# Moving the dots of the adaLN parameters between the stages of a two-layer decoder trunk

## The chip, the cores and the metric

The kernel runs on one core of one Trainium2 chip. A core has TensorE (PE; its weight loads, shown apart as PEld, overlap the products), VectorE (DVE), ScalarE (ACT), GpSimd (POOL) and SyncE (SP, which here only issues DMAs). The metric is device microseconds (us) of one execution; a kernel's time is the median of its runs.

## The reference

Two layers work on x of 512 positions by 1024 features, float32, one sequence. Both parts of a layer start with an RMS norm that is scaled and shifted by parameters computed from a vector c (adaLN):

```python
c_act = silu(c)
for l in range(2):
    mod = (c_act @ w_ada + b_ada)[:, None, :]
    sh1, sc1, g1, sh2, sc2, g2 = jnp.split(mod, 6, axis=-1)       # 1024 values each
    h = rmsnorm(x, norm1_w) * (1 + sc1) + sh1
    u = h @ w_in
    u_pool, u_conv, b_conv, c_conv, q, k, v, gate_logits = jnp.split(u, offsets, axis=-1)
    y_pool = pool_mixer(u_pool, pool_w, pool_scale)               # 256 wide
    y_conv = b_conv * causal_short_conv(c_conv * u_conv, conv_w)  # 256 wide
    q, k = rope(rmsnorm(q)), rope(rmsnorm(k))                     # 8 heads of 64
    o = moba_attention(q, k, v)                                   # blocks of 256 keys
    gates = sigmoid(gate_logits)                                  # 3 x 1024
    merged = (gates[:, :, 0] * (y_pool @ p_pool) + gates[:, :, 1] * (y_conv @ p_conv)
              + gates[:, :, 2] * (y_attn @ p_attn))
    x = x + g1 * (merged @ w_out)
    h2 = rmsnorm(x, norm2_w) * (1 + sc2) + sh2
    x = x + g2 * ((silu(h2 @ w_gate) * (h2 @ w_up)) @ w_down)     # 2816 wide
```

Each of the six parameters of a layer is a vector of 1024 sums over 1024 products. Sc1 and sh1 are wanted when the layer starts, g1 by the projection after the gates, sc2 and sh2 by the second norm, g2 by the first down projection.

## The kernel before

**Layout and products.** Activations lie feature by position: x is eight tiles of 128 features by 512 positions. A float32 product is made of three products of rounded halves: each operand is split into a rounded part and the rest (hi and lo), and `mm3` issues hi x hi, hi x lo and lo x hi into one accumulator (`matmul`, L149). There are four single accumulators in PSUM (`ps_mm`) and two double ones (`ps_pair`). All matmuls and some other instructions are pinned in program order; the rest the Tile framework's scheduler may move on their engine.

**The weights** come as one stream in a planned order, eight 128x128 blocks (512 KB) at a time. `next_w` keeps up to `ahead_now` of them loaded ahead. `load_w` has SP issue the DMA (L232) into a tile named `raw`, of which there are three (`RAW`); ACT copies the rounded part (L325, `whi`) and DVE subtracts (L328, `wlo`), five buffers each. The split frees the raw tile, a matmul frees whi and wlo. In the feed-forward part, gate and up weights are summed in memory by POOL's accumulating DMAs (L254, L256) into tiles named `w`, of which there are six; they are then split by the same two lines.

**The dots.** The adaLN parameters are not made on PE. For 128 values at a time `ada_step` has SP load 512 KB of `w_ada`, transposed on the host, and DVE multiplies by silu(c) and sums along the row in one instruction (L374). Its tile is a raw one where `early` is true, else a w one (`w4`). `ada_tasks` lists the eight dots of a part, at a cost of 1.2 each, and `ada_end`, at 0.2, which adds the bias and, for a scale, folds in the norm's weight. Layer 0's scale and shift 1 are computed apart (`ada_first`), at the start.

**The order of work** is written by hand around PE. Each 2048 output columns of matmuls (four `mm3` of 512) make one `tick()`. A tick advances the `fibers` (attention) and runs tasks from a queue, `bulk`, by a credit that grows by `bulk_rate[0]` with each tick; `flush_bulk()` runs all that is left:

```python
def ada_step(l, part, j, early):
    aw = wp.tile([P, D], F32, tag="raw", name=nm("raw"), bufs=RAW) if early else w4([P, D])
    nc.sync.dma_start(aw, ada[l, part, j])
    pin(ada_dot(aw, l, part, j))
...
gains = ada_tasks(l, (G1,)) if l > 0 else []
bulk.extend(gains[:4])
k_ps = wide()
...
bulk.extend(ada_tasks(l, (G1, SC2, SH2)[l:], True))
bulk_rate[0] = (0.5, 0.35)[l]
```

**The stages of a layer**, with what runs as bulk in them:

- *The loop along k* (L723 to L744) makes q and the first three of the six pool and convolution tiles, and goes along the contraction because the norm's output comes one feature tile at a time. In layer 1 `second()` (L738) finishes the norm of the second half of the positions.
- *Convolution, k and v*: three products by `feature_tile`, then `wide()` twice, for k and for v. The pool and convolution chains run as bulk on DVE; `flush_bulk()` ends the convolution's, k's and v's part. In layer 1 the eight dots of G1 are here (L849): four in k's part, four in v's.
- *Convolution and pool products* (L888 to L899): the convolution's first tile, two pool products, the convolution's second tile. L890 multiplies the first into the convolution's output, `cv`.
- *Gates and attention* (L901 on): 24 gate products, each through Tanh (L909) and `gated` (L914), with the products of the three branches; attention's units run between them as fibers. A unit is 128 queries of a pair of heads: scores, maxima and gate sums on DVE (L602 to L610), exponentials on ACT (L612, L614), scaling on DVE (L616 to L619), transposes on PE (L155), products with v. As bulk run, in early (raw) tiles, 24 dots in layer 0 (G1, SC2, SH2, at a rate of 0.5) and 16 in layer 1 (SC2, SH2, at 0.35).
- *The projection* with `tail`, adding to x by L954 (`residual`), with the dots of G2 as bulk in w tiles.
- *Feed-forward* in four parts, `PARTS` (L47): products of gate and up, most of them in pairs by a Strassen-Winograd scheme (`glu_pair`, Silu in L1087 to L1089), then the part's down products, added to x by L954. At the start of each down stage the bulk rate is set to 1.5, and halfway through it to 0. Part 0 of layer 0 holds the dots of layer 1's SC1 and SH1 (L1126); parts 1 and 2 hold none. The last part's down products run in `tail` with layer 1's first norm (L1139 to L1146).

Of the kernel before, what the change touches and what calls it, by code (L numbers as in the profile page):

```python
# [24 lines left out]
L = 2  # L25
# [21 lines left out]
PARTS = ((3, 1, 1), (0, 0, 3), (0, 0, 2), (0, 0, 3))  # L47

SUMS_AHEAD = 4

RAW, BIG = 3, 46

# [5 lines left out]
SH1, SC1, G1, SH2, SC2, G2 = range(6)  # L58
# [19 lines left out]
def hybrid_trunk(ctx, tc, xT, ws, ada, cols, pool_w, qk_w, crow, pos, con, out):  # L78
    nc = tc.nc
    V, A, T = nc.vector, nc.scalar, nc.tensor  # L80
# [20 lines left out]
    def ps_mm():  # L101
        return psum.tile([P, S], F32, tag="mm", name=nm("mm"), bufs=4)
# [16 lines left out]
    bulk = deque()  # L119
    bulk_rate, credit = [0.0], [0.0]  # L120
# [23 lines left out]
    def drain():  # L144
        while fibers:
            tick()
# [202 lines left out]
    def next_w(ahead=None):  # L349
        ahead = ahead_now[0] if ahead is None else ahead  # L350
        while at[0] < len(items) and len(loaded) <= ahead:
            loaded.append(load_w())
        return loaded.popleft()
# [55 lines left out]
    def ada_tasks(l, parts, early=False):  # L409
        out = []  # L410
        for part in parts:
            for j in range(KT):
                out.append((1.2, lambda part=part, j=j: ada_step(l, part, j, early)))
            out.append((0.2, lambda part=part: ada_end(l, part)))
        return out
# [90 lines left out]
    def split_from(src, scale=None):  # L506

        hi, lo = bigt(), bigt()
        if scale is None:
            A.activation(hi, src, AF.Copy)  # L510
            V.tensor_sub(lo, src, f32(hi))  # L511
        else:
            A.activation(hi, src, AF.Copy, scale=scale)
            V.scalar_tensor_tensor(lo, src, scale, f32(hi), op0=ALU.mult, op1=ALU.subtract)
        return hi, lo

    def second(nrm, l, i, bank):

        hold[0] = None
        nrm.stat(BLOCK, S, bank)  # L520
        for k, lo, hi in HALVES[3:] + REST:
            nrm.apply(l, i, k, lo, hi)
# [192 lines left out]
    for l in range(L):  # L715
# [7 lines left out]
        for n, (k, lo, hi) in enumerate([(k, 0, S) for k in range(KT)] if l == 0 else HALVES + REST):  # L723
            if l == 0:
                if k + 3 < KT:
                    first.append(ada_first_load(k + 3))
                if k + 2 < KT:
                    ada_first(k + 2, first[k + 2], SC1)
                    ada_first(k + 2, first[k + 2], SH1)
                    norm.first_scaled(k + 2)  # L730
                    norm.first_hi(k + 2)
                loaded.append(load_w())
                if k + 2 < KT:
                    norm.first_lo(k + 2)
            if k not in held:
                held[k] = next_w(0 if l == 0 else None)
            if l > 0 and n == 1:
                second(norm, l, 0, bank)  # L738
            w = held[k]
            h = norm.k(k)  # L740
            for t in range(lo // P, hi // P):
                mm3(q_ps[t], cut(h, slice(None), slice(t * P, (t + 1) * P)), wrow(w, 0), k == 0, k == KT - 1)
            for z in range(3):
                mm3(f_ps[z][:, lo:hi], wblk(w, 4 + z), cut(h, slice(None), slice(lo, hi)),  # L744
                    k == 0 and lo == 0, k == KT - 1)
# [8 lines left out]
        def feature_tile(o, w):  # L754
            for k in range(KT):
                mm3(o, wblk(w, k), norm.k(k), k == 0, k == KT - 1)
# [56 lines left out]
        cv = {}  # L813
# [32 lines left out]
            if j == 1:  # L846
                bulk.append((0, lambda: pool_chain(1, pool1)))

        gains = ada_tasks(l, (G1,)) if l > 0 else []  # L849
        bulk.extend(gains[:4])  # L850
        k_ps = wide()
        for t in range(TT):
# [32 lines left out]

        m01, y_attn = [], []
        fibers.append([3, attention(l, qk, v, nrq, prq, y_attn)])
        pb = ps_mm()  # L888
        feature_tile(pb, next_w())
        V.tensor_mul(cv[0], pb, cv[0])  # L890
        y_conv.append(split_from(cv[0]))
        for j in range(2):
            pp = ps_mm()
            mm3(pp, (pw["h"][:, j, :], pw["l"][:, j, :]), pooled[j], True, True)
            y_pool.append(split_from(pp, scale=col(C_PS + j)))
        pb = ps_mm()
        feature_tile(pb, next_w())
        V.tensor_mul(cv[1], pb, cv[1])
        y_conv.append(split_from(cv[1]))  # L899

        bulk.extend(ada_tasks(l, (G1, SC2, SH2)[l:], True))  # L901
        bulk_rate[0] = (0.5, 0.35)[l]
        ahead_now[0] = 3

        def gate():
# [190 lines left out]
        for part, (along, single, pairs) in enumerate(PARTS):  # L1096
            act = []
            nk = along + single + 2 * pairs
            if along:
                held = {}  # L1100
                for n, (k, lo, hi) in enumerate(HALVES + REST):
                    if n == 1:
                        second(norm, l, 1, bank)
                        table(AF.Silu, norm.y[:, 0:1])
                    if k not in held:
                        held[k] = next_w()
                    for z in range(2 * FA):
                        mm3(f_ps[z][:, lo:hi], wblk(held[k], z), cut(norm.k(k), slice(None), slice(lo, hi)),
                            k == 0 and lo == 0, k == KT - 1)
                    if k >= HK:  # L1110
                        make_forms(k - HK)
                del held
                for z in range(FA):
                    glu(f_ps[z], f_ps[FA + z])
            for _ in range(single):
                wg = next_w()
                g = ps_mm()
                feature_tile(g, wg)
                u = ps_mm()
                feature_tile(u, next_w())  # L1120
                glu(g, u)
            bulk_rate[0] = 0.0
            for _ in range(pairs):
                glu_pair()
            if part == 0 and l + 1 < L:
                bulk.extend(ada_tasks(l + 1, (SC1, SH1)))  # L1126
            bulk_rate[0] = 1.5
            blk = Blocks(nk, 4)
            if part + 1 < len(PARTS):
                for n in range(KT):  # L1130
                    if n == KT // 2:
                        bulk_rate[0] = 0.0
                    o = ps_mm()
                    for k in range(nk):
                        mm3(o, blk(n, k), act[k], k == 0, k == nk - 1)
                    residual(n, o, 0, S, G2)
            elif l + 1 == L:
                tail(lambda k: act[k], blk, G2, nk, None, True)
            else:  # L1139
                flush_bulk()  # L1140
                drain()
                n1 = Norm()
                table(AF.Abs_reciprocal_sqrt, f32(act[-1][1])[:, 0:1])
                scratch = ps_pair()
                bank = scratch[:, 1]
                tail(lambda k: act[k], blk, G2, nk, n1, False, lead(n1, l + 1, 0, bank), 4)  # L1146
                norm = n1
# [100 lines left out]
```

## Time and profile before

| | |
|---|---|
| time, median of 3 runs | 1480.35 us |
| lowest and highest | 1479.25 and 1482.27 us |
| the profiled execution | 1480.46 us |
| its span in the profile | 1478.7 us |
| ACT and POOL busy | 666.3 us (45%), 105.8 us (7%) |
| DMA | 217.19 MB, 147 GB/s on average |

The span goes from the first instruction to the last; the time of the execution holds some 1.8 us around it. All times within the kernel are from the start of the span.

A row of a timeline gives start, length, engine, line, operation, output and inputs with their form and a count (instructions of one kind behind one another are drawn together). In brackets stand the idle time of the engine ahead of it and who ended it. "mm" and "pair" are accumulators, "big" a tile of 128x512, "tmp" a scratch tile, "in_ws" the stream of weights in memory, "in_ada" the transposed w_ada. Rows that sum the waits give engine, tile and line, releaser, and then total, number and largest. A table of windows gives, for each stretch, its length and each engine's busy time with its instructions, then the granted clock of TensorE (1.00 is full speed), the share of the DMA engines and GB/s. A row of the DMA issues gives queue, count, size and the time from issue to landing.

DVE's largest groups by line are the weight splits (L328), 284.7 + 86.7 us from raw and from w tiles, the dots (L374), and the residuals (L954) with 62.0 us; ACT's largest are the splits' first halves (L325), 248.8 + 76.2 us.

### The profile page before, as it was taken

The page shows a single profiled execution, that of the slowest core. Times are in us where ns is not written, and L with a number is a line of the kernel's source. Part 1 is how long each engine was busy: PE and PEld are TensorE (multiplying, and loading weights), DVE is VectorE, ACT ScalarE, POOL GpSimd, SP SyncE. Part 2 cuts the span into 40 slices and gives each one's busy share as a digit, 9 for nine tenths or more (in the row PEclk, how much of TensorE's full clock was granted, in tenths as well). Part 3 has the DMA queues.
Part 4 walks back from the last instruction along what each step waited for, and adds up shares of the span by engine and source line. Part 5 has one row for each costly group of instructions (what it writes and reads, how often), then busy time and mean ns, then how long its engine had stood idle before and what let it go on. Part 6 is the DMA issues. An engine that isn't in the chain of part 4 may idle for free.

```text
span 1478.7 us, 21940 instructions
## 1 busy us (share of the span) xinstructions
PE 1456.7 (99%) x8443; PEld 1268.0 (86%) x8443; DVE 1052.2 (71%) x1855; ACT 666.3 (45%) x1138; POOL 105.8 (7%) x157
## 2 busy tenths in 40 slices
PE   8999999999999999999999999999999999999999
PEld 6888787778988998989988877778889889989997
DVE  7976887758686876767666777776586757657672
ACT  4634555443453352535444345455335525434350
POOL 0000000001100211210000000000010102111200
PEclk9999999999999999999999999999999999999999
DMA  9514433365337775744334443333462436637431
GB/s 346 199 73 159 141 136 134 115 227 148 109 114 221 207 190 174 198 113 117 114 109 146 155 143 126 102 114 128 143 193 81 141 114 167 191 89 196 131 105 65
DMA packets 84409, 217.19 MB, mean 147 GB/s; under 512 B 10832, under 2 KB 23760, under 8 KB 84304
## 3 DMA queue, kind: packets, MB, share of 16 engines
q1 hardware_dynamic: 67456, 177.37, 35.2%
q0 software_dynamic: 16128, 37.76, 11.6%
q8 instruction: 66, 1.08, 0.3%
q10 hardware_dynamic: 720, 0.66, 0.1%
q14 instruction: 39, 0.32, 0.1%
HBM read 213.65 MB, written 2.10 MB: 146 GB/s over the span
## 4 chain that ended last, share of the span: by engine, by line
PE 84%; DVE 8%; DMA 3%; ACT 3%; issue 1%; SPq 0%; DVEq 0%; ACTq 0%
PE mm L149 72%; PE pair L149 11%; DMA raw<-in_ws 2%; DVE wlo L328 2%; PE mm L155 1%; ACT whi L325 1%; DMA w<-in_ada 1%; DVE w L374 1%; DVE raw L374 1%; ACT tmp L612 0%; DMA x<-in_xT 0%; ACT tmp L614 0%; DVE big L914 0%; SPq L232 0%; DVE big L929 0%
## 5 line engine op out<-in xcount | busy, mean ns | idle before, releaser
L149 PE MATMUL mm<-big,whi 128*128 128x512 f32 (+1 forms) x4362 | 1083.3, 340 | 5.6 <-DVE tmp L1081 2.5
L149 PEld LDWEIGHTS mm<-big,whi 128*128 128x128 f32 x4362 | 746.0, 190 | 93.6 <-DVE tmp L1081 4.1
L149 PE MATMUL mm<-big,wlo 128*128 128x512 f32 (+1 forms) x2181 | 736.1, 337 | 0.0
L149 PEld LDWEIGHTS mm<-big,wlo 128*128 128x128 f32 x2181 | 413.9, 190 | 44.7
L325 ACT ACTIVATE whi<-raw 128x1024 fp32r<-128x1024 f32 (+2 forms) x240 | 248.8, 1039 | 298.3 <-PE mm L149 231.1
L328 DVE TENSOR_TENSOR wlo<-raw,whi 128x1024 fp32r<-128x1024 f32 (+2 forms) x240 | 284.7, 1193 | 81.9 <-ACT whi L325 81.0
L325 ACT ACTIVATE whi<-w 128x1024 fp32r<-128x1024 f32 x72 | 76.2, 1059 | 147.8 <-PE mm L149 107.7
L954 DVE SCALAR_TENSOR_TENSOR x<-mm,mod,x 128x512 f32<-128x512 f32 (+1 forms) x90 | 62.0, 689 | 101.4 <-PE mm L149 101.3
L254 POOL DMA_DIRECT2D w<-in_ws x72 | 48.5, 683 | 982.1 <-DVE w L374 377.3
L328 DVE TENSOR_TENSOR wlo<-w,whi 128x1024 fp32r<-128x1024 f32 x72 | 86.7, 1220 | 31.0 <-ACT whi L325 30.2
L149 PE MATMUL pair<-whi,big 128*128 128x512 f32 x224 | 76.7, 390 | 0.0
L256 POOL DMA_DIRECT2D w<-in_ws x72 | 64.6, 923 | 153.1 <-DMA w<-in_ws 136.3
L149 PE MATMUL pair<-big,whi 128*128 128x256 f32 (+1 forms) x376 | 74.0, 294 | 0.0
L374 DVE SCALAR_TENSOR_TENSOR w<-w,csil 128x1024 f32<-128x1024 f32 x56 | 66.9, 1220 | 9.5 <-DMA w<-in_ada 9.3
L149 PEld LDWEIGHTS pair<-big,whi 128*128 128x128 f32 x376 | 60.4, 191 | 2.2
L149 PE MATMUL mm<-whi,big 128*128 128x512 f32 x160 | 57.2, 394 | 1.7 <-ACT big L497 1.4
L149 PE MATMUL pair<-big,wlo 128*128 128x256 f32 (+1 forms) x188 | 55.3, 294 | 0.0
L511 DVE TENSOR_TENSOR big<-tmp,big 128x512 fp32r<-128x512 f32 x48 | 33.0, 690 | 24.3 <-ACT big L510 23.4
L149 PEld LDWEIGHTS pair<-whi,big 128*128 128x128 f32 x224 | 42.1, 188 | 8.7
L374 DVE SCALAR_TENSOR_TENSOR raw<-raw,csil 128x1024 f32<-128x1024 f32 x40 | 48.4, 1218 | 1.2 <-DMA raw<-in_ada 1.2
L914 DVE SCALAR_TENSOR_TENSOR big<-big,mm 128x512 f32<-128x512 f32 x48 | 32.6, 682 | 21.5 <-PE mm L149 21.1
L149 PE MATMUL pair<-wlo,big 128*128 128x512 f32 x112 | 43.6, 390 | 0.0
(187 smaller groups left out, 1251.5 us busy)
## 6 DMA issues: line engine op xcount, KB each, us to landing
raw<-in_ws SPq DMA_DIRECT2D x146, 512.0 KB, 3.4
w<-in_ws POOLq DMA_DIRECT2D x144, 256.0 KB, 4.6
w<-in_ada SPq DMA_DIRECT2D x56, 512.0 KB, 5.3
raw<-in_ada SPq DMA_DIRECT2D x40, 512.0 KB, 3.2
raw<-in_ws SPq DMA_DIRECT2D x64, 256.0 KB, 4.2
raw<-in_ws SPq DMA_DIRECT2D x24, 384.0 KB, 3.5
raw<-in_ws SPq DMA_DIRECT2D x16, 448.0 KB, 5.3
raw<-in_ws SPq DMA_DIRECT2D x36, 128.0 KB, 3.0
```

The source lines that it names most:

```text
L149: tc.keep_in_program_order(T.matmul(*a, **k))
L155: tc.keep_in_program_order(T.transpose(*a))
L254: nc.gpsimd.dma_start(dst, self.source(0, 1))
L256: nc.gpsimd.dma_start(dst, self.source(*other), accum_op=ALU.add)
L325: A.activation(hi[:, :n], raw[:, :n], AF.Copy)
L328: ins = V.tensor_sub(lo[:, :n], raw[:, :n], f32(hi)[:, :n])
L374: return V.scalar_tensor_tensor(aw, aw, 1.0, csil, op0=ALU.mult, op1=ALU.mult, accum_out=mod[l][:, part, j:j + 1])
L511: V.tensor_sub(lo, src, f32(hi))
L914: V.scalar_tensor_tensor(sg, sg, 1.0, branch, op0=ALU.add, op1=ALU.mult)
L954: V.scalar_tensor_tensor(x[k][:, lo:hi], src, mod[l][:, part, k:k + 1], x[k][:, lo:hi], op0=ALU.mult, op1=ALU.add)
```

## The change

Dots move to other stages, and the convolution and pool products change places:

- G1's eight dots of layer 0 go from the gate stage into the k and v stage, in w tiles, as they already are in layer 1. Layer 0's gate stage keeps SC2's and SH2's 16, at a rate of 0.35 in place of 0.5.
- The 16 dots of layer 1's SC2 and SH2 go from layer 1's gate stage into w tiles earlier in the program: the first five (`AHEAD2`) into the down stage of part 2 of layer 0, the other three of SC2 with its `ada_end` into the last down stage of layer 0, at a rate of 0.8, and SH2's eight into layer 1's loop along k, behind `second()`, at 0.6. Layer 1's gate stage has none left.
- The order convolution 0, pool 0, pool 1, convolution 1 becomes convolution 0, pool 0, convolution 1, pool 1. The weights' order in the stream stays.

No product, dot or transfer is added or taken away.

```diff
--- before.py
+++ after.py
@@ -47,6 +47,7 @@
 PARTS = ((3, 1, 1), (0, 0, 3), (0, 0, 2), (0, 0, 3))
 
 SUMS_AHEAD = 4
+AHEAD2 = 5
 
 RAW, BIG = 3, 46
 
@@ -736,6 +737,8 @@
                 held[k] = next_w(0 if l == 0 else None)
             if l > 0 and n == 1:
                 second(norm, l, 0, bank)
+                bulk.extend(later)
+                bulk_rate[0] = 0.6
             w = held[k]
             h = norm.k(k)
             for t in range(lo // P, hi // P):
@@ -846,7 +849,7 @@
             if j == 1:
                 bulk.append((0, lambda: pool_chain(1, pool1)))
 
-        gains = ada_tasks(l, (G1,)) if l > 0 else []
+        gains = ada_tasks(l, (G1,))
         bulk.extend(gains[:4])
         k_ps = wide()
         for t in range(TT):
@@ -885,21 +888,18 @@
 
         m01, y_attn = [], []
         fibers.append([3, attention(l, qk, v, nrq, prq, y_attn)])
-        pb = ps_mm()
-        feature_tile(pb, next_w())
-        V.tensor_mul(cv[0], pb, cv[0])
-        y_conv.append(split_from(cv[0]))
         for j in range(2):
+            pb = ps_mm()
+            feature_tile(pb, next_w())
+            V.tensor_mul(cv[j], pb, cv[j])
+            y_conv.append(split_from(cv[j]))
             pp = ps_mm()
             mm3(pp, (pw["h"][:, j, :], pw["l"][:, j, :]), pooled[j], True, True)
             y_pool.append(split_from(pp, scale=col(C_PS + j)))
-        pb = ps_mm()
-        feature_tile(pb, next_w())
-        V.tensor_mul(cv[1], pb, cv[1])
-        y_conv.append(split_from(cv[1]))
-
-        bulk.extend(ada_tasks(l, (G1, SC2, SH2)[l:], True))
-        bulk_rate[0] = (0.5, 0.35)[l]
+
+        if l == 0:
+            bulk.extend(ada_tasks(l, (SC2, SH2), True))
+        bulk_rate[0] = 0.35
         ahead_now[0] = 3
 
         def gate():
@@ -1122,8 +1122,13 @@
             bulk_rate[0] = 0.0
             for _ in range(pairs):
                 glu_pair()
-            if part == 0 and l + 1 < L:
-                bulk.extend(ada_tasks(l + 1, (SC1, SH1)))
+            if l + 1 < L:
+                if part == 0:
+                    bulk.extend(ada_tasks(l + 1, (SC1, SH1)))
+                    later = ada_tasks(l + 1, (SC2, SH2))
+                elif part == 2:
+                    bulk.extend(later[:AHEAD2])
+                    del later[:AHEAD2]
             bulk_rate[0] = 1.5
             blk = Blocks(nk, 4)
             if part + 1 < len(PARTS):
@@ -1139,6 +1144,9 @@
             else:
                 flush_bulk()
                 drain()
+                bulk.extend(later[:4])
+                del later[:4]
+                bulk_rate[0] = 0.8
                 n1 = Norm()
                 table(AF.Abs_reciprocal_sqrt, f32(act[-1][1])[:, 0:1])
                 scratch = ps_pair()
```

## The prediction, made before the changed kernel ran

> **What bounds the kernel now.** I read the page first, then the busy times by stage, then what TensorE (PE) waits for, and last the rows of the other engines ahead of each wait. The page:
>
> ```profile
> span 1478.7 us, 21940 instructions
> ...
> PE 1456.7 (99%) x8443; PEld 1268.0 (86%) x8443; DVE 1052.2 (71%) x1855; ACT 666.3 (45%) x1138; POOL 105.8 (7%) x157
> ...
> L374 DVE SCALAR_TENSOR_TENSOR w<-w,csil 128x1024 f32<-128x1024 f32 x56 | 66.9, 1220 | 9.5 <-DMA w<-in_ada 9.3
> ...
> L374 DVE SCALAR_TENSOR_TENSOR raw<-raw,csil 128x1024 f32<-128x1024 f32 x40 | 48.4, 1218 | 1.2 <-DMA raw<-in_ada 1.2
> ...
> w<-in_ada SPq DMA_DIRECT2D x56, 512.0 KB, 5.3
> raw<-in_ada SPq DMA_DIRECT2D x40, 512.0 KB, 3.2
> ```
>
> PE works through 1456.7 of 1478.7 us, so the change, which adds and removes no matmul, has 22.0 us of PE idle time to play with. A dot costs DVE 1.22 us and SP one transfer of 512 KB; there are 96 dots before and after. They only move, so all that counts is what waits behind them in the old place and in the new one. By stage (layer 0: conv to v, gates with attention, down stage of part 2, last down stage; layer 1: loop along k, gates with attention), PE busy stands behind the length:
>
> ```profile
> core 0: us, PE busy (x) PEld busy (x) DVE busy (x) ACT busy (x) POOL busy (x), PEclk, DMA share, GB/s
> 55.00:122.00 67.00, 67.00 (x297) 55.52 (x296) 50.35 (x117) 31.11 (x50) 0.31 (x1) 1.00 0.35 119
> 122.00:318.00 196.00, 191.95 (x992) 153.99 (x992) 151.69 (x351) 98.13 (x215) 0.00 (x0) 1.00 0.43 147
> 628.00:651.00 23.00, 22.31 (x99) 17.99 (x98) 12.34 (x18) 5.08 (x6) 0.00 (x0) 1.00 0.28 89
> 714.00:743.00 29.00, 29.00 (x186) 26.48 (x184) 16.43 (x29) 9.96 (x17) 0.00 (x0) 1.00 0.22 69
> 743.00:783.00 40.00, 40.00 (x216) 34.70 (x215) 24.96 (x39) 16.37 (x24) 0.00 (x0) 1.00 0.34 114
> 853.00:1048.00 195.00, 189.37 (x974) 152.63 (x974) 142.05 (x333) 96.69 (x214) 0.00 (x0) 0.99 0.38 131
> ```
>
> The two gate stages hold 4.05 + 5.63 = 9.68 us of idle PE, nearly half of all; the stages that receive dots hold 0.69 together. Dots take this much of DVE in the two gate stages (each counts twice, with the read of its sum):
>
> ```profile
> 122.00:318.00 196.00, 29.23 (x48) 1.00 0.43 147
> 853.00:1048.00 195.00, 19.46 (x32) 0.99 0.38 131
> ```
>
> So 24 dots in layer 0 and 16 in layer 1; the change leaves 16 and none. These are PE's waits there: the rows with a bracket give the idle time before the matmul and who ended it, the last three are the sums by releaser in 122 to 318 us.
>
> ```profile
> 303.94 1.07 PE L155 MATMUL mm<-ident,tmp 128*128 128x128 f32 x8 [1.87 <-DVE tmp L619]
> ...
> 854.12 0.70 PE L149 MATMUL mm<-big,whi 128*128 128x512 f32 x2 [1.11 <-DVE big L890]
> ...
> 891.02 0.85 PE L155 MATMUL mm<-ident,tmp 128*128 128x128 f32 x6 [0.98 <-DVE tmp L619]
> ...
> 943.12 1.65 PE L149 MATMUL mm<-w,big 128*128 128x256 f32 x6 [2.36 <-ACT big L909]
> ...
> 991.78 1.06 PE L155 MATMUL mm<-ident,tmp 128*128 128x128 f32 x8 [1.18 <-DVE tmp L619]
> ...
> PE mm L155 <- DVE tmp L619: 2.5, 3, 1.9
> PE mm L149 <- DVE big L914: 1.2, 1, 1.2
> PE mm L155 <- DVE big L514: 0.3, 1, 0.3
> ```
>
> Layer 1's four are 1.11 + 0.98 + 2.36 + 1.18 = 5.63, all of its idle time. In layer 0 the 1.87 is one of the three waits for L619; 2.13 remain.
>
> **The change part by part.** *Dots out of the softmax chain.* A transpose waits for L619, the end of a chain: the maxima and gate sums on DVE (L602 to L610), exponentials on ACT (L612, L614), the scaling (L616 to L619). Ahead of the wait of 1.87:
>
> ```profile
> 297.52 1.22 DVE L328 TENSOR_TENSOR wlo<-raw,whi 128x1024 fp32r<-128x1024 f32 x1
> ...
> 298.72 1.22 DVE L374 SCALAR_TENSOR_TENSOR raw<-raw,csil 128x1024 f32<-128x1024 f32 x1
> ...
> 297.86 1.07 ACT L325 ACTIVATE whi<-raw 128x1024 fp32r<-128x1024 f32 x1 [2.69 <-DMA raw<-in_ws]
> ...
> 300.25 0.57 ACT L612 ACTIVATE tmp<-pair,asm,nrq 128x256 f32<-128x256 f32 x1 [1.32 <-DVE asm L610]
> ...
> 884.87 1.22 DVE L374 SCALAR_TENSOR_TENSOR raw<-raw,csil 128x1024 f32<-128x1024 f32 x1
> ```
>
> A weight split and a dot stand inside the chain, 2.4 us (the fourth row shows the exponential waiting 1.32 us for DVE). In the built order of the changed kernel this last unit (pair 3, row 3) has neither: 1.87 go. The unit before the wait of 0.98 loses its dot, the last row, 1.22 against 0.98: it goes. The one of 1.18 has no dot in its chain but loses a split and a product from it in the new order; I take half, 0.6 of 0 to 1.18.
>
> *Dots out of the raw buffers.* The wait of 2.36 is another mechanism:
>
> ```profile
> 933.08 1.23 DVE L328 TENSOR_TENSOR wlo<-raw,whi 128x1024 fp32r<-128x1024 f32 x1
> ...
> 934.38 0.33 SPq L232 DMA_DIRECT2D raw<-in_ws  x1
> ...
> 938.75 1.06 ACT L325 ACTIVATE whi<-raw 128x1024 fp32r<-128x1024 f32 x1 [3.77 <-DMA raw<-in_ws]
> ...
> 942.46 0.61 ACT L909 ACTIVATE big<-mm 128x512 f32<-128x512 f32 x1
> ...
> ACT whi L325 <- DMA raw<-in_ws: 14.3, 8, 3.8
> ...
> raw<-in_ws SPq DMA_DIRECT2D x146, 512.0 KB, 3.4
> ```
>
> The three raw buffers are shared by weights and dots, so the weight's transfer is issued only when the split at 933.08 has ended (934.3), and lands when ACT has waited 3.77 us for it. Behind that split stand the exponentials and the Tanh (L909) that frees the accumulator PE wants. ACT's waits of this kind sum to 14.3 us in layer 1's gate stage (last row but one: sum, number, largest). From issue to ACT's start are 938.75 - 934.38 = 4.4 us here, and 3.4 is the page's median. Without dots the third buffer is free one dot or more earlier, and that dot itself need not be landed before it, so I take the whole 2.36 away. It has a second price:
>
> ```profile
> 942.80:946.20 3.40, 3.08 (x10) 2.77 (x11) 3.40 (x7) 1.22 (x3) 0.00 (x0) 0.50 0.03 11
> ```
>
> The granted clock is 0.50 for 3.40 us right after it: 3.08 us of matmuls at half speed, 1.54 us lost. The Trainium skill (TensorE: Matmul & The Clock Gate, "What's actually happening") says that the clock halves after an idle window of about 3.4 us. Here 2.36 us of idle time were enough, so the trace goes further than the page; by the page this halving would not count and the sum would end 1.54 higher.
>
> *Alternation.* The convolution's second product comes ahead of the second pool product. Rows ahead of the wait of 1.11:
>
> ```profile
> 852.15 1.21 DVE L328 TENSOR_TENSOR wlo<-raw,whi 128x1024 fp32r<-128x1024 f32 x1
> 853.29 0.68 DVE L890 TENSOR_TENSOR big<-mm,big 128x512 f32<-128x512 f32 x1
> ```
>
> With four accumulators, the second convolution product comes fifth and needs the first one's, which L890 reads late. In the new order it is third and takes one of v's; the second pool product, behind v's tile, takes the old one. The 1.11 go.
>
> *What is added.* Eight dots of G1 in layer 0 between 55 and 122 us: 9.8 us on a DVE that is busy 50.35 of 67. Their cover is that weights are split far ahead, five buffers deep:
>
> ```profile
> ACT whi L325 <- PE mm L149: 12.2, 5, 4.4
> ```
>
> In 55 to 122 us the splitter waits 12.2 us for PE to free a buffer and never for a transfer. If the cover were gone, a delayed split would cost 1.22 each; I take 0. Only two w buffers are free there, so each pair of transfers waits on SP for the pair of dots before, with weights queued behind: some 5.3 + 2.4 us, which five split weights cover. Five dots go into part 2's down stage (12.34 of 23 busy), three into the last (16.43 of 29), eight into layer 1's loop (24.96 of 40): PE's accumulators there wait for L954, which comes at most three dots (3.7 us) late. Part 2's eight output products take 23 us, 2.9 each, and with four accumulators a late one is wanted three products, 8.6 us, on: 0. One place is not covered, the end of part 2's pairs:
>
> ```profile
> 626.52 1.06 ACT L325 ACTIVATE whi<-raw 128x1024 fp32r<-128x1024 f32 x1 [1.85 <-DMA raw<-in_ws]
> 627.48 0.37 ACT L1089 ACTIVATE tmp<-mm 128x256 f32<-128x256 f32 x1
> ```
>
> ACT already waits 1.85 us for a weight, with the last Silu (L1089) behind it, and PE then idles 0.69. Two dots' transfers are now issued a few weights ahead of this one on SP. Bounds: nothing (they end before it starts) and 2 x 5.3 = 10.6. The weight's issue waits for a split much later than theirs, so I take 0.3, near the lower end. In layer 0's gate stage one unit (pair 2, row 2) gains a dot in its chain: 0 to 1.22, I take 0.6.
>
> *The sum.* -1.87 - 0.98 - 0.6 - 2.36 - 1.54 - 1.11 + 0.3 + 0.6 = -7.56 us. The profiled execution took 1480.46 (span 1478.7), close to the median of 1480.35, so 1472.9.
>
> **The rivals.** *The idle time stays under other names.* Splits (1.22 each) and gate products remain in the chains, and the exact order decides; layer 0 with 24 dots idles less (4.05) than layer 1 with 16 (5.63), so dots alone do not make it. Then only the alternation and the clock are won, 1.11 + 1.54 = 2.65: 1477.8, within 0.2%. Against it: both chains above hold a dot or its buffer by name.
>
> *The transfers moved ahead on SP (slower).* At 626.5 the two dots' loads are served fully before the weight: 10.6 us later at ACT, and PE idles by all of it: 1472.9 - 0.3 + 10.6 = 1483.2, and slower by more than 0.2% as soon as layer 0's k and v stage adds any. It decides from about 8 us of delay. For it: the 1.85 us wait is there already. Against it: DMA is busy 0.28 in that stage. The Trainium skill (DMA: Bandwidth & Descriptors, "Queues, rings and completion order") says that each ring takes descriptors in order, so a dot ahead delays a weight; no row here separates that from SP's own order.
>
> *More than forecast.* All 9.68 us and the 1.54 go: 1480.46 - 11.2 = 1469.2. For it, layer 1's gate stage has no dot left; against it, layer 0 keeps 16 and the waits for L914 and L514.
>
> **How the numbers follow.** Forecast 0.66, stays 0.14, slower rival 0.07, more 0.13. The range runs from 1469.2, all known idle time, to 1480.4, no gain. A measurement of this kernel tells 0.2% (2.96 us) from no change: under 1477.4 is faster, over 1483.3 slower. Faster: the forecast and the last rival, 0.79. Within: 0.14. Slower: 0.07.
>
> **What would show it.** Right: PE idle in layer 1's gate stage under 2 us, no wait of ACT there for a weight's transfer above 1 us, the granted clock at 1.00 throughout it, no PE wait for L890; layer 0's about 2 to 3 us. PE full in 55 to 122 and in layer 1's loop. Wrong: idle PE at 629 well above 0.69, a wait for a transfer between 55 and 122, or the gate stages at 8 us and more.

## The result

The changed kernel takes 1470.6 us (median of 4 runs, 1468.3 to 1472.6) against 1479.8 us for the kernel before (4 runs, 1478.97 to 1482.27). The ratio is 0.9935, with a 95% interval of 0.9914 to 0.9955. The forecast of 1472.9 lies 2.3 us above the median and inside its range. A second session, with five runs, gave 1472.45 us and a ratio of 0.9943 (0.9930 to 0.9957).

The profiled execution of the changed kernel took 1469.42 us, that of before 1480.46. The page has these lines now; the dots in raw tiles fall from 40 to 16, so 80 are in w tiles:

```profile
span 1467.6 us, 21944 instructions
...
PE 1454.1 (99%) x8443; PEld 1267.3 (86%) x8443; DVE 1055.0 (72%) x1855; ACT 665.3 (45%) x1138; POOL 106.0 (7%) x157
...
L375 DVE SCALAR_TENSOR_TENSOR w<-w,csil 128x1024 f32<-128x1024 f32 x80 | 95.6, 1220 | 12.1 <-DMA w<-in_ada 11.7
...
w<-in_ada SPq DMA_DIRECT2D x80, 512.0 KB, 4.9
```

(One line was added at the top of the file, so L374 of before is L375 here.) PE idles 1467.6 - 1454.1 = 13.5 us, 8.5 less than before. The same stages by busy time, with bounds moved to where their matmuls now lie (layer 0: conv to v, gates, part 2's down stage, the last down stage; layer 1: loop, gates), and below them DVE's dots in the two gate stages:

```profile
55.00:122.00 67.00, 67.00 (x297) 55.47 (x296) 57.25 (x130) 30.01 (x46) 0.31 (x1) 1.00 0.54 182
122.00:313.00 191.00, 190.81 (x992) 154.24 (x991) 145.36 (x338) 98.69 (x218) 0.00 (x0) 1.00 0.40 136
624.00:646.50 22.50, 22.47 (x101) 18.29 (x100) 16.69 (x26) 5.20 (x6) 1.99 (x3) 1.00 0.60 184
709.50:738.50 29.00, 29.00 (x186) 26.48 (x185) 19.84 (x37) 10.09 (x17) 0.00 (x0) 1.00 0.37 123
738.50:778.50 40.00, 40.00 (x216) 34.70 (x215) 34.12 (x56) 16.36 (x24) 0.00 (x0) 1.00 0.42 140
847.00:1037.30 190.30, 189.01 (x982) 152.21 (x981) 127.21 (x299) 97.38 (x216) 0.00 (x0) 1.00 0.26 92
...
122.00:313.00 191.00, 19.44 (x32) 1.00 0.40 136
847.00:1037.30 190.30, 0.00 (x0) 1.00 0.26 92
```

Layer 0's gate stage idles 0.19 us (4.05 before), layer 1's 1.29 (5.63 before), and the granted clock is 1.00 there. The stages that received dots have DVE busier (57.25 against 50.35, 34.12 against 24.96) and PE as full as before. What is left of PE's waits in the two gate stages, and of the splitter's waits for a weight's transfer (15.8 us in layer 0 and 14.3 in layer 1 before; only layer 0 has any now):

```profile
PE mm L150 <- DVE big L914: 0.2, 1, 0.2
...
PE mm L150 <- ACT big L909: 0.5, 1, 0.5
PE mm L150 <- DVE asm L617: 0.5, 1, 0.5
PE mm L150 <- DVE w L632: 0.3, 1, 0.3
...
ACT whi L326 <- DMA raw<-in_ws: 4.4, 4, 2.0
```

No wait for L619, L514 or L890 is left. Both traces hold the same 8443 matmuls, nearly all in the same order, so the start of a matmul in one can be subtracted from its start in the other; where the difference steps, time was won or lost. A step is often 0.1 to 0.3 us larger than the wait that the trace shows there. These are the steps, by stage, of several kernels against the profiled execution of before (negative: won):

```
stage of before, us      changed  alternation  layer 1  G1 moved  no dots in
                                  alone        moved              layer 1's gates
0 to 122                 -0.16    -0.11        +0.51    -0.04     -0.16
122 to 318 (gates 0)     -4.90    +2.63        +2.13    -4.63     +0.37
493 to 587 (part 1)      +1.40    +1.14        +0.01    +1.25     +1.15
628 to 651 (part 2)      -0.89    -0.89        -0.93    -0.91     -0.89
651 to 714 (part 3)      +0.01    +0.01        +0.89    +0.02     +0.01
783 to 853 (L890)        -1.49    -1.55        -0.54    -0.30     -0.01
853 to 1048 (gates 1)    -4.71    -2.26        -4.70    -1.48     -4.75
```

Every kernel that was profiled wins 0.9 at 630 us, whether it changes anything ahead of there or not, and most lose 0.9 to 2.1 in part 1. Those two rows thus belong to the one execution of before that was profiled, not to the change. The forecast argued from that execution's 0.69 us at 629.

### The profile page after: what moved, and what is told of

It is laid out like the page before. It is cut to its first block, busy times and chain, and to the rows that moved or that the text cites. A ratio compares the mean times of both kernels' runs of the same rounds, so it can differ in the third digit from the quotient of the medians.

```text
span 1467.6 us, 21944 instructions
## 1 busy us (share of the span) xinstructions
PE 1454.1 (99%) x8443; PEld 1267.3 (86%) x8443; DVE 1055.0 (72%) x1855; ACT 665.3 (45%) x1138; POOL 106.0 (7%) x157
## 4 chain that ended last, share of the span: by engine, by line
PE 89%; DVE 4%; DMA 3%; ACT 2%; issue 1%; SPq 0%; POOL 0%; DVEq 0%; ACTq 0%; POOLq 0%
PE mm L150 76%; PE pair L150 11%; PE mm L156 2%; DMA w<-in_ada 1%; DVE wlo L329 1%; ACT whi L326 1%; DMA w<-in_ws 1%; DVE w L375 1%; DMA raw<-in_ws 1%; DMA x<-in_xT 0%; DVE tmp L1081 0%; DVE big L515 0%; DVE tmp L1090 0%; DVE tmp L482 0%; ACT tmp L613 0%
## 5 line engine op out<-in xcount | busy, mean ns | idle before, releaser
L375 DVE SCALAR_TENSOR_TENSOR w<-w,csil 128x1024 f32<-128x1024 f32 x80 | 95.6, 1220 | 12.1 <-DMA w<-in_ada 11.7
L914 DVE SCALAR_TENSOR_TENSOR big<-big,mm 128x512 f32<-128x512 f32 x48 | 32.6, 684 | 26.4 <-PE mm L150 26.1
L511 ACT ACTIVATE big<-tmp 128x512 fp32r<-128x512 f32 x48 | 29.6, 620 | 19.7 <-DVE tmp L809 10.6
```

The source lines that it names most:

```text
L375: return V.scalar_tensor_tensor(aw, aw, 1.0, csil, op0=ALU.mult, op1=ALU.mult, accum_out=mod[l][:, part, j:j + 1])
L914: V.scalar_tensor_tensor(sg, sg, 1.0, branch, op0=ALU.add, op1=ALU.mult)
```

## The experiments

**Each part alone.** First the order of the products, with the dots left in place:

```diff
-        pb = ps_mm()
-        feature_tile(pb, next_w())
-        V.tensor_mul(cv[0], pb, cv[0])
-        y_conv.append(split_from(cv[0]))
         for j in range(2):
+            pb = ps_mm()
+            feature_tile(pb, next_w())
+            V.tensor_mul(cv[j], pb, cv[j])
+            y_conv.append(split_from(cv[j]))
...
```

> The kernel before, with the order of convolution and pool products alternating and nothing else changed. My theory: only the wait for L890 at 854 us (1.11 us, a shift of 1.4 us between the two traces) goes, and the gate stages keep their 4.05 and 4.5 us of idle time and the halved clock at 943: 1.1 to 1.4 us less, about 1478.5. Rival, the idle time goes by the exact order alone: the swap shifts every later task by one place and takes 3 us or more out of the gate stages, dots or not.

Measured: 1479.22 us (11 runs), ratio 0.9994 (0.9981 to 1.0006). The step at 854 us is there (-1.55), as expected, but in the time of the whole kernel nothing can be seen. Layer 0's gate stage took 2.63 us more in the profiled execution: 1.0 for a wait of 0.89 at 162 us, which also stands (with 0.26 to 0.53) in four kernels below that keep the old order, and 1.6 for a halved clock at 305 us, of which more at the end. The rival fell: the swap takes nothing out of a gate stage by order, and its -2.26 in layer 1 is the same wait shortened from 2.36 to 1.5 us with the clock unhalved.

**Layer 1's dots alone**:

```diff
+                    later = ada_tasks(l + 1, (SC2, SH2))
...
-        bulk.extend(ada_tasks(l, (G1, SC2, SH2)[l:], True))
+        if l == 0:
+            bulk.extend(ada_tasks(l, (G1, SC2, SH2), True))
```

> The kernel before, with layer 1's SC2 and SH2 dots moved to layer 0's down stages and layer 1's loop; G1 of layer 0 and the order of the products stay. My theory: layer 1's gate stage falls from 5.63 to about 1.1 (L890) + 1.3 us of idle time and the clock stays at 1.00, the receiving stages stay full: 4 to 5.5 us less, about 1475. Rival, the exact order: layer 1's idle time comes back under other names, 1.5 us less at most. Rival, transfers on SP: idle time at the end of part 2's pairs rises above 1 us.

Measured: 1476.0 us (12 runs), ratio 0.9982 (0.9973 to 0.9992). In layer 1's gate stage 4.70 us go and the clock stays at 1.00; part 2's down stage is as full as elsewhere. The medians differ by 3.3 us, where 4 to 5.5 was expected. In the profiled execution (1477.39 us) layer 0's gate stage, in which this kernel changes nothing, took 2.13 us more: 0.5 for the wait at 162 us and 1.6 for a halved clock at 305. Part 3's first pair lost 0.89 us, which neither theory had.

**G1 alone**:

```diff
-        gains = ada_tasks(l, (G1,)) if l > 0 else []
+        gains = ada_tasks(l, (G1,))
...
-        bulk.extend(ada_tasks(l, (G1, SC2, SH2)[l:], True))
-        bulk_rate[0] = (0.5, 0.35)[l]
+        bulk.extend(ada_tasks(l, (SC2, SH2), True))
+        bulk_rate[0] = 0.35
```

> The kernel before, with layer 0's G1 dots moved to the k and v stage and the rate 0.35 in both gate stages; layer 1's dots and the order of the products stay. My theory: layer 0's gate stage falls from 4.05 to under 1 us of idle time and its k and v stage stays full: 3 to 4.5 us less, about 1476; layer 1 as before (5.6 us and the halved clock). Rival, the exact order: without the alternation layer 0's idle time stays above 2.5 us.

Measured: 1474.41 us (6 runs), ratio 0.9965 (0.9953 to 0.9977). Layer 0's gate stage is at 0.2 us of idle time without any alternation. The three ratios sum to 0.06 + 0.18 + 0.35 = 0.59% less, beside the 0.65 and 0.57% of the whole change: within their intervals, the parts add up.

**Layer 1's dots left out**, in place of moved:

```diff
-        bulk.extend(ada_tasks(l, (G1, SC2, SH2)[l:], True))
+        if l == 0:
+            bulk.extend(ada_tasks(l, (G1, SC2, SH2), True))
+        else:
+            ada_end(l, SC2)
```

> The kernel before, with layer 1's SC2 and SH2 dots left out (their sums are taken as zero, so scale and shift of the second norm are left out in part). It shows what layer 1's gate stage is without dots where nothing receives them. My theory, that the receiving stages cost nothing: within 0.8 us of the kernel that moves these dots, 4 to 5.5 us less than before. Rival, that receiving them costs 1 us or more: faster than that kernel by as much.

Measured: 1475.9 us (7 runs), ratio 0.9973 (0.9962 to 0.9983), not to be told from the kernel that moves them (1476.0 us, 0.9982), and the gate stage wins 4.75 us beside 4.70 there. So receiving these 16 dots costs nothing that the times can show; a small cost is found below.

**DVE's time or the raw buffers.** Two kernels take the dot of layer 1's gate stage apart. The first keeps the instruction and drops its load and buffer:

```diff
+        if early and l == 1:
+            pin(V.scalar_tensor_tensor(csil, csil, 1.0, csil, op0=ALU.mult, op1=ALU.max,
+                                       accum_out=mod[l][:, part, j:j + 1]))
+            return
         aw = wp.tile([P, D], F32, tag="raw", name=nm("raw"), bufs=RAW) if early else w4([P, D])
```

> The kernel before, with layer 1's 16 gate-stage dots kept on DVE at full size but without their loads and without a raw buffer (they read silu(c) instead, so scale and shift of layer 1's second norm are not the reference's). It keeps DVE's time and takes the raw buffers' share away. My theory of two mechanisms: the wait of 2.36 at 943 and the halved clock behind it go (3 to 3.5 us together), the one of 0.98 at 891, a dot in a softmax chain, stays: about 3 us less. Rival, DVE time alone: both waits stay and nothing is won. Rival, buffers alone: all that the kernel without dots won in this stage, 4.7 us, goes here too.

The second keeps load and buffer and cuts the instruction:

```diff
         nc.sync.dma_start(aw, ada[l, part, j])
+        if early and l == 1:
+            pin(V.scalar_tensor_tensor(aw[:, :16], aw[:, :16], 1.0, csil[:, :16], op0=ALU.mult, op1=ALU.mult,
+                                       accum_out=mod[l][:, part, j:j + 1]))
+            return
```

> The kernel before, with layer 1's 16 gate-stage dots cut to 16 of their 1024 columns while their loads and raw buffers stay (so scale and shift of layer 1's second norm are sums over 16 products). It takes DVE's time away and keeps the transfers and the raw buffers. My theory of two mechanisms: the wait at 891 goes (1.0 us), most of the wait at 943 stays, since the weight's transfer still waits for a raw buffer that a dot holds: 1 to 2 us less. Rival, DVE time alone: all 4.7 us of the kernel without dots go.

Measured: 1476.67 (11 runs) and 1476.69 us (11 runs), ratios 0.9981 (0.9973 to 0.9990) and 0.9982 (0.9974 to 0.9991). By the times, then, either alone wins about as much as moving the dots (0.9982), and the second kernel wins more than the 1 to 2 us that were expected of it; how the gain divides rests on one profiled execution of each. In these, of 4.75 us without any dot, 3.35 go with the load and 4.34 with the instruction. In each of the three, 1.4 of this is the halved clock, which none of them has. The timeline ahead of the wait at 943 us shows the buffer's part. With loads and tiny dots (the stage lies at nearly the same times):

```profile
933.10 0.33 SPq L232 DMA_DIRECT2D raw<-in_ws  x1
...
937.03 1.07 ACT L325 ACTIVATE whi<-raw 128x1024 fp32r<-128x1024 f32 x1 [3.14 <-DMA raw<-in_ws]
...
941.40 0.98 PE L149 MATMUL mm<-w,big 128*128 128x256 f32 x6 [1.73 <-ACT big L913]
```

and with full dots and no loads:

```profile
937.64 1.06 ACT L325 ACTIVATE whi<-raw 128x1024 fp32r<-128x1024 f32 x1 [1.96 <-PE mm L149]
...
942.02 0.98 PE L149 MATMUL mm<-w,big 128*128 128x256 f32 x6 [0.56 <-ACT big L913]
```

Where a dot holds a raw tile, ACT still waits 3.14 us for the weight's transfer with DVE nearly free of dots, and PE waits 1.73. Where no dot holds one, ACT waits only for PE to free a buffer. So of the 2.36, 0.6 goes with DVE's time alone and 1.8 with the loads alone; 0.56 is left without the loads, and 0.54 in the changed kernel. The wait at 991 us is DVE's alone: 1.2 with full dots and no loads, gone with tiny dots. The wait of 0.98 at 891 went in both, against the expectation that it stays with full dots: the dot there runs 0.5 us earlier although that execution is 1.7 us later at this point. It takes both causes; how they meet was not followed further.

**Number or spacing.** G1 moved, with layer 0's rate left at 0.5:

```diff
-        bulk.extend(ada_tasks(l, (G1, SC2, SH2)[l:], True))
+        bulk.extend(ada_tasks(l, (SC2, SH2), True))
         bulk_rate[0] = (0.5, 0.35)[l]
```

> The kernel with G1's dots of layer 0 in the k and v stage, but with the old rates (0.5 in layer 0, 0.35 in layer 1): 16 dots, spaced as the 24 were. The number of dots falls as in the kernel with G1 moved, their spacing doesn't change. My theory, that a stall comes where two dots meet one softmax chain: at 0.5 the first 16 dots stay dense and the waits of 2.2 us at 247 to 261 us stay at least in part, while the one of 1.87 at 304 goes, for no dot is left there: 2 to 3 us less than before, 1.5 to 2.5 us above the kernel with 0.35. Rival, the number alone counts: the same as with 0.35, 4.6 us less in this stage.

Measured: 1474.92 us (8 runs), ratio 0.9974 (0.9962 to 0.9985). This expectation failed: the stage wins 3.87 us, and of the waits between 247 and 261 nothing is left. The trace of before shows why; the first two rows are PE, the others DVE:

```profile
247.36 0.85 PE L155 MATMUL mm<-ident,tmp 128*128 128x128 f32 x6 [0.42 <-DVE tmp L619]
...
256.58 0.98 PE L149 MATMUL mm<-w,big 128*128 128x256 f32 x6 [1.23 <-DVE big L914]
...
240.88 0.16 DVE L369 SCALAR_TENSOR_TENSOR am<-mod,colt 128x8 f32<-128x8 f32 x1
...
248.62 1.22 DVE L374 SCALAR_TENSOR_TENSOR raw<-raw,csil 128x1024 f32<-128x1024 f32 x1
...
254.63 1.22 DVE L374 SCALAR_TENSOR_TENSOR raw<-raw,csil 128x1024 f32<-128x1024 f32 x1
```

L369 folds SC2 into the norm's weight, after the sixteenth dot. So 16 dots had run by 240.88 us with no PE wait at all, and every wait of the stage, 0.42 at 247 first among them, lies among the last eight. At 254.63 the second of two dots stands right ahead of L914, which frees PE's accumulator. With 16 dots at the old rate none comes after 241 (the last stands at 237.2). With the new rate three do, in the changed kernel at 252.0, 268.7 and 277.6 us: the first stands right ahead of L914 again and costs 0.19 us, the others nothing. In these traces, then, it is what a dot stands ahead of that counts, and neither the number of dots nor their spacing alone.

**The change without the alternation:**

```diff
-        for j in range(2):
-            pb = ps_mm()
-            feature_tile(pb, next_w())
-            V.tensor_mul(cv[j], pb, cv[j])
...
+        pb = ps_mm()
+        feature_tile(pb, next_w())
+        V.tensor_mul(cv[0], pb, cv[0])
...
```

> The changed kernel with the old order of the convolution and pool products (both moves of dots kept). My theory: the wait for L890 in layer 1 comes back, 1.0 to 1.5 us over the changed kernel, about 1472, and layer 0's gate stage stays under 1 us of idle time. Rival, the orders interact: without the alternation the waits of the gate stages come back too, 3 us or more over the changed kernel. Rival, the alternation is worth nothing: the same time.

Measured: 1471.17 us (5 runs), ratio 0.9945 (0.9933 to 0.9956). L890's wait of 1.1 us is back and costs 1.6 in the step between the two profiled executions; the gate stages stay at 0.5 and 1.3 us. In time, the alternation is below what the runs tell apart.

**The changed kernel again**, for the variation from one execution to the next:

> The changed kernel once more, for a second profile and more times. My theory: the gate stages are again under 0.5 and under 1.6 us idle, the part 1 wait for L1081 near 506 us varies with the execution and is not the change's, and the time is 1470 to 1471. Rival: the low idle time was one execution's luck, and a wait of 1 us or more stands again in a gate stage.

Measured: 1472.45 us (5 runs), where 1470 to 1471 was expected. Gate stages as in the first profile (0.2 and 1.3 us). But part 3's first pair waits 0.7 us for L1081, 0.95 us in the step of that stage, as in the kernel with layer 1's dots alone.

**Twice the dots in the receiving stages:**

```diff
+        if (l, part) in ((0, G1), (1, SC2), (1, SH2)):
+            pin(V.scalar_tensor_tensor(csil, csil, 1.0, csil, op0=ALU.mult, op1=ALU.max,
+                                       accum_out=mod[l][:, part, j:j + 1]))
         pin(ada_dot(aw, l, part, j))
```

> The changed kernel with a second instruction of a dot's size in front of each of the 24 moved dots (it reads silu(c) and needs no load; the first dot's result is overwritten, but silu(c) is replaced by the larger of itself and itself, which leaves it as it is). It doubles DVE's part of what the receiving stages took. My theory, that weights split five deep and late residuals cover it: 29 us more on DVE, 0 to 1.5 us more in time. Rival, the cover is already used up: each extra dot costs up to its 1.22, 8 us or more, with idle PE in 55 to 122 us, at 630 to 651 and in layer 1's loop.

Measured: 1478.69 us (11 runs), ratio to before 0.9988 (0.9977 to 0.9999): 6.2 us over the changed kernel of the same session, where 0 to 1.5 was expected. The profiled execution, with 1475.68 us the fastest of the 11, lies 3.7 us over the profiled one of that kernel, and shows where:

```profile
126.35 0.70 PE L150 MATMUL mm<-big,whi 128*128 128x512 f32 x2 [2.30 <-ACT big L887]
...
668.43 0.80 PE L150 MATMUL mm<-big,whi 128*128 128x256 f32 x2 [3.56 <-DVE tmp L1084]
...
663.77 0.69 DVE L263 TENSOR_TENSOR w<-w,raw 128x512 f32<-128x512 f32 x1 [3.86 <-DMA w<-in_ws]
```

(Lines below the edit lie three lower than in the changed kernel, but for those above it, such as L263.) Layer 1's loop paid nothing. Behind v, the copy of v (L887) that frees the accumulators came late. Part 3's first pair paid most, 3.56 us of waiting and then a halved clock. Its cause is neither a late split nor the SP queue that the slower rival spoke of: DVE's sum of weights for the Strassen-Winograd products (L263) waits 3.86 us for GpSimd's transfers into w tiles, the tiles that the dots in the down stage ahead of it use. GpSimd's first transfer for part 3 started at 611.0 us in the kernel before, and starts at 638.5 in the changed kernel and at 645.8 here. The next two kernels test whether the dots are the reason.

**No dots in part 2** (AHEAD2 = 0 in place of 5):

```diff
-AHEAD2 = 5
+AHEAD2 = 0
```

> The changed kernel with no dots in part 2's down stage (AHEAD2 = 0): four of SC2 in the last down stage, twelve dots in layer 1's loop and what follows it. My theory, that the transfers moved ahead of part 2's last weight cost nothing: idle PE at the end of part 2's pairs and in the down stage stays as in the changed kernel, and the loop, with twelve dots in place of eight, costs 0 to 1.2 us more. Rival, the transfers on SP cost up to 0.5 us there: that much less at 624 to 634 us.

Measured: 1469.7 us (4 runs), ratio 0.9918 (0.9904 to 0.9931), beside 0.9943 for the changed kernel in the same session (and 0.9935 in the first, whose interval overlaps). GpSimd's first transfer for part 3 starts at 607.4 us again, 31 us earlier than with the five dots. At 624 to 634 us nothing differs, so the forecast's 0.3 us there was nothing. Part 3 has no wait above 0.3, and the loop carries twelve dots for nothing. One wait of this kind remains, in part 1, behind the dots of SC1 and SH1 in part 0's down stage. (Ten of the 16 run there, up to 483.1 us; the trace shows the other six in part 1's down stage, from 553.9 to 568.7 us, so part 1 is not without dots.) These are PE's wait, and GpSimd's first transfers for part 1 with the dots as releaser:

```profile
506.50 0.51 PE L150 MATMUL mm<-big,whi 128*128 128x256 f32 x2 [0.99 <-DVE tmp L1081]
...
483.73 0.57 POOL L255 DMA_DIRECT2D w<-in_ws  x1 [43.11 <-DVE w L375]
484.88 0.56 POOL L255 DMA_DIRECT2D w<-in_ws  x1 [0.58 <-DVE w L375]
...
501.84 0.69 DVE L263 TENSOR_TENSOR w<-w,raw 128x512 f32<-128x512 f32 x1 [1.30 <-DMA w<-in_ws]
```

**SC1's and SH1's dots spread**, to test that:

```diff
-                    bulk.extend(ada_tasks(l + 1, (SC1, SH1)))
+                    ones1 = ada_tasks(l + 1, (SC1, SH1))
+                    bulk.extend(ones1[:9])
...
+                elif part == 1:
+                    bulk.extend(ones1[9:13])
                 elif part == 2:
-                    bulk.extend(later[:AHEAD2])
-                    del later[:AHEAD2]
+                    bulk.extend(ones1[13:])
```

> The kernel with none of SC2's and SH2's dots in part 2 (AHEAD2 = 0), and layer 1's 16 dots of SC1 and SH1 spread: eight stay in part 0's down stage, four go to part 1's, four to part 2's. My theory, that dots in w tiles hold back GpSimd's sums for the next part's first pair: GpSimd's first sum for part 1 is loaded 5 us earlier or more against the stage, the PE wait for L1081 near 505 us (1.0 to 1.3 us in the last three kernels) goes, and parts 2 and 3 gain at most 0.4 us each of such a wait: 0.3 to 1.2 us less than with AHEAD2 = 0 alone in the profiled execution. Rival, that wait belongs to part 1's first pair itself: it stays at 1 us or more, and the time is the same.

Measured: 1468.15 us (5 runs, 1467.24 to 1468.92), ratio 0.9916 (0.9902 to 0.9929). Of this kernel, GpSimd's first transfers, and DVE's sum:

```profile
477.19 0.57 POOL L255 DMA_DIRECT2D w<-in_ws  x1 [36.21 <-DVE w L375]
479.10 0.56 POOL L255 DMA_DIRECT2D w<-in_ws  x1 [1.34 <-DVE w L375]
...
500.93 0.69 DVE L263 TENSOR_TENSOR w<-w,raw 128x512 f32<-128x512 f32 x1
```

They begin 6.5 us earlier, the sum waits for nothing, PE's wait at 505 us is gone, and the step against the kernel with AHEAD2 = 0 is -1.24 us in part 1 and within 0.04 in parts 2 and 3. So dots in w tiles do hold GpSimd back; that is shown by the start of its transfers in both tests. Whether PE then waits varies: with ten dots in part 0's down stage, nine of thirteen profiled executions have the wait in part 1 (0.6 to 1.8 us), and four, that of before among them, have none, so one execution without it would be weak evidence by itself. In time nothing is shown: the ratio is that of AHEAD2 = 0 (0.9918), though this kernel has the lowest median of the study.

## Why the prediction was right, step by step

- *Dots out of the softmax chains, layer 0* (-1.87 and +0.6, so -1.27): right in kind, far too small. The step is -4.90, and -4.63 with G1 alone. The forecast left 2.13 us of waits at 247 to 261 us standing without looking into them, though the same dots stood in them; and the unit of pair 2, row 2 that gains a dot pays nothing for it. The wait that was counted gave 2.03, those left standing 2.38, and the rest lies in steps under 0.2. This is the term that was mis-sized, by 3.6 us. The sign that was to show it, 2 to 3 us of idle time left in this stage, failed the same way: 0.19 are left.
- *Layer 1's chains and raw buffers* (-0.98, -0.6, -2.36): the waits at 891 and 991 gave 1.02 and 1.34, the one at 943 with small steps ahead of it 2.06 (0.54 stays under the same name), and 0.82 came back at 987, where a wait for L617 appears, and 0.35 at 950 (L632). Sum -3.25 against -3.94. That raw buffers, and not only DVE's time, make the 2.36 is shown by the two kernels that part load and instruction.
- *The clock* (-1.54): the halving at 943 went, 1.40 in the steps. But the kernel before pays it only in some executions (below), so as a term of the median it was too certain.
- *Alternation* (-1.11): the wait went, 1.49 in the steps; alone it can't be seen in the time.
- *Receiving stages at nothing*: right for the amount moved, not for the reason given. The cover of the weight splits was nearly used up behind v, as the doubled dots show. And the +0.3 at 626 us was argued from a wait that only this one execution of before had.
- *Missed*: dots in w tiles hold back GpSimd's weight sums for the next part's first pair. The changed kernel pays 0 to 0.95 us for it in part 3. The waits of before had the sign of it, which this row sums over the whole kernel:

```profile
POOL w L254 <- DVE w L374: 377.3, 4, 300.8
```

The 300.8 is GpSimd's idle time before the first feed-forward part and says little; two of the other three waits, 42.7 and 33.3 us, stand ahead of parts 1 and 2, and there it is the dots that end them.

The two profiled executions differ by 11.04 us, where 7.56 was forecast; the medians differ by 9.2 and 8.4 us. The three parts alone and the whole agree, so the gain is that of the dots' places. The first rival (the idle time stays under other names) and the slower one (transfers on SP) both fell; most of the idle time of the gate stages went, as in the last rival, except 0.19 + 1.29 us. That rival, given 0.13, came nearer than the forecast: its 1469.2 us lies 1.4 from the first median and 0.2 from the profiled execution, the forecast 2.3 and 3.5. The direction and the mechanisms named were right; that the medians differ by only 0.8 to 1.6 us more than was forecast is in part luck, since the 3.6 us missed in layer 0 are partly covered by what the forecast did not have: 1.40 us lost in part 1, and runs of before that do not pay for the clock.

## What to carry to other kernels

Filler work on a half-idle engine is placed by what waits behind it, not by the engine's load: moving layer 1's 16 dots won 4.7 us (1.4 of it the clock's) in a gate stage where DVE was busy 142.05 of 195 us, and eight of them cost nothing in a loop where they made it 34.12 of 40. Each such task also takes a buffer from a ring, and whoever shares the ring waits (weights on SP for raw tiles, GpSimd's sums for w tiles), so the releaser named in the waits of an idle queue is worth reading. And a wait under 1 us that stands in one profiled execution is no ground for a term until another kernel that shares the stage shows it too.

## What was not expected of the hardware

Whether a wait of about 2 us halves the clock hangs on where it falls. Ahead of the same transposes, the kernel before waited 1.87 us (the row at 303.94) and the kernel with the alternation alone 1.93, almost the same. Of before:

```profile
301.12:304.53 3.41, 1.54 (x11) 1.07 (x10) 1.86 (x7) 2.41 (x8) 0.00 (x0) 1.00 0.75 255
...
304.00:307.40 3.40, 3.40 (x20) 2.92 (x21) 1.30 (x5) 1.92 (x4) 0.00 (x0) 1.00 0.30 119
```

and of the alternation alone:

```profile
304.86 1.78 PE L155 MATMUL mm<-ident,tmp 128*128 128x128 f32 x8 [1.93 <-DVE tmp L619]
...
301.64:305.06 3.42, 1.49 (x8) 0.98 (x7) 1.48 (x6) 2.81 (x10) 0.00 (x0) 1.00 0.92 275
...
305.20:308.40 3.20, 3.20 (x12) 2.82 (x11) 1.03 (x4) 1.94 (x4) 0.00 (x0) 0.50 0.24 95
```

The granted clock stayed at 1.00 in the first and fell to 0.50 in the second, for 3.41 us. Other waits look as arbitrary: those of 1.97 (layer 1's dots moved), 2.36, 2.49 and 3.56 us were followed by 3.41 us at 0.50 too, and those of 2.08, 2.30 and another 1.97 (layer 1's dots left out) were not.

The traces hold the reason. In each of them the granted clock changes only at points a whole number of 3.413 us apart, to 0.001 us: with layer 1's dots moved it falls at 18.84 and at 305.56 us, 84 such stretches apart, and in before at 942.83 and, behind the last matmul, at 1478.72, 157 apart. Cut the fourteen traces into these stretches, and PE's busy time in one goes with the clock in the next. Behind the first 20 us, the clock fell from 1.00 after every stretch with 1.49 us of busy PE or less, and after none with 1.54 or more; the first rows of the two fences above are the two nearest to that bound. (At 15 us, two stretches with 1.61 and 1.77 were followed by a low one.) The 1.97 that cost a halving lay whole within one stretch, and the 1.97 that did not was cut into 1.79 and 0.18; 2.08 and 2.30 were cut too. Where the stretches lie against the work differs from one execution to the next, so a wait near 2 us costs some 1.5 us more in one execution and not in another. Of 25 runs of before in one session, 11 had a mean granted clock of 1.000, with a median of 1478.3 us, and 14 a lower one, with 1480.9. The Trainium skill (TensorE: Matmul & The Clock Gate, "What's actually happening") lets the clock fall after an idle window of about 3.4 us; the stretches here have that length, but one with 1.49 us of busy PE in it was enough.
